# A two-layer decoder trunk: the steps of the mixers in a new order, the first loads and casts rearranged, and a few small operations rewritten

## The chip, the cores and the metric

The kernel runs on one core of a Trainium2 chip. The metric is device time in microseconds (us), the median of several executions. The engines are TensorE (PE, its weight loads PEld), VectorE (DVE), ScalarE (ACT), GpSimd (POOL) and SyncE (SP), which here issues loads and stores.

## The reference

The input is 256 rows of 1024 numbers, all in fp32. Two layers follow each other, each with two sub-layers. With `mod = silu(c) @ w_ada + b_ada`, split into shift, scale and gate for each sub-layer:

```
h = rms_norm(x, g_pre_mix) * (1 + sc1) + sh1
q, k, v, pz = split(h @ w_in)                     # 512 columns each
ao = causal attention, 8 heads of 64, partial rotary (one block of 256)
po = pool_scale * (windowed causal means of pz, minus pz) @ w_pool, 4 groups
y = concat(rms_norm(ao), rms_norm(po)) @ w_out
x = x + gt1 * rms_norm(y, g_post_mix)
h = rms_norm(x, g_pre_ffn) * (1 + sc2) + sh2
a, g = split(causal width-3 conv of (h @ w_up))   # 2816 columns each
x = x + gt2 * rms_norm((silu(a) * g) @ w_down, g_post_ffn)
```

## The kernel before, in words

Rows are in two blocks of 128 (`b` is 0 or 1), columns of a result in two halves (`hf`). Each matmul of full precision is three matmuls of split operands: an operand is cast to a high part (`hi` of a weight, by ACT; `hh` of an activation) and DVE subtracts it from the original for the low part (`lo`, `hl`); `mm3` adds hi*hi, lo*hi and hi*lo.

Weights come through `Stream`: SP issues the loads in one fixed order, each into one of four raw slots of 128 x 2048 numbers, as soon as the slot four units back is free (`pump`, `free`). The parts have eight buffers each for `hi` and `lo` (`high`, `low`, `ahead`). Some weights are not split: the shift and scale columns of `w_ada` (`w_a1`, `w_s2`) are dot products on DVE against `cbc`, the broadcast silu(c); the gate columns (`w_gt`) are matmuls of PE.

The start loads `c` (`row`), x, the identity, the first small vectors and the first weights, all on SP. DVE makes the mean squares of both blocks of x, POOL the power -1/2, DVE the normalised rows `xn`. In `mixer` for layer 0, PE transposes `xn` (`T`), ACT copies the banks to `xT`, and then for each of 8 chunks of 128 input columns `chunk(k)` makes two dot products (`ada1`), a coefficient (`pre_coef`), the casts of the chunk's `w_in` (two parts), and `hh`, `h` and `hl` (`Normed.make`), after which PE runs 24 matmuls (`w_in`). The work of chunk k + 1 stands ahead of the matmuls of chunk k.

`steps` holds what follows in a mixer, as steps of two letters and numbers, issued on each engine in the order of the written list `ORDER[l]`. An engine takes its steps in that order and waits at each for its inputs:

- `cq`, `ck`, `cv`, `cz` copy the projection out of PSUM (a capital letter puts the copy on ACT), `ro` is the rotary (DVE), `kq` transposes (PE), `tq` copies them (`tQ` on ACT);
- `sc` scores (PE), `mx` mask and maximum (DVE), `ex` exponentials (ACT), `rc` and `nm` normalise (DVE; `nM` on ACT), `pt` transposes the probabilities (PE), `cp` copies them (ACT), `at` multiplies with v (PE);
- `wi`, `cd`, `po` are the pooled half (PE, ACT, PE); `mh`, `ml`, `sq`, `sa` split and square both halves; `yP` and `wo` are the output projection of the pooled and the attention half (PE), `cy` copies the former's sum (ACT);
- `ss`, `r1`, `r2` give the two norms' factors (PE, DVE, POOL), `ad` adds the two sums with the factor (DVE), `yq` squares (ACT), `yG` multiplies with factor and gate (DVE), `ry` is the norm's factor (POOL), `xu` updates x (DVE), `xs`, `rx`, `xN` do the same for the next norm (ACT, POOL, DVE), `tr` transposes (PE);
- `gp`, `gq` are the gate and shift columns (PE), `gr`, `gs` copy them, `gc`, `gd` transpose them, `gm`, `gn` add the bias, `gt`, `gg` spread a gate over the rows; `s2` is a dot product (DVE); `hi`, `lo` are casts of weights to come; `tx` and `ts` load ACT's function table for Exp and Silu.

`rstd` on POOL adds eps to the first half's mean square, adds the second half's and takes the power. `ffn` follows, with its own casts, then `tail` (the same chain of norms) and the second layer. The mixer's list ends where the feed-forward net's matmuls (`u`) begin; they need `hl`, `hh` and the first four parts of `w_up`.

Of the kernel before, what the change touches and what calls it, by code (L numbers as in the profile page):

```python
# [76 lines left out]
class Stream:  # L77
# [13 lines left out]
    def add(self, src, n, cuts=()):  # L91
        i = len(self.units)
        self.units.append((src, n))
        self.done.append(False)
        for j, (a, b) in enumerate(cuts):
            self.cut(i, a, b, j == len(cuts) - 1)
        return i
# [4 lines left out]
    def pump(self):  # L102
        while self.loaded < len(self.units):
            src, n = self.units[self.loaded]
            t = None
            if not isinstance(n, int):
                self.nc.sync.dma_start(n, src)
            elif len(self.slots) < RAW_BUFS or self.done[self.slots[-RAW_BUFS]]:
# [54 lines left out]
def trunk(ctx: ExitStack, tc: tile.TileContext, x, c, ct, vec, ident_d, tab_d, w_a1, w_gt, w_s2, w_g2,  # L163
# [80 lines left out]
    for j in range(8):  # L244
        if j:
            add_a1(0, j)
        else:
            A1[0, 0] = [st.add(*h) for h in by_half(w_a1[0, 0])]
# [864 lines left out]
```

## Time and profile before

| | us |
|---|---|
| median of 3 runs (610.43 to 611.44) | 610.45 |
| the profiled execution's own time | 611.41 |
| its span, first to last instruction | 609.6 |
| busy: PE, PEld | 584.1, 504.0 |
| busy: DVE, ACT, POOL | 490.4, 376.7, 29.8 |

Busy time adds up an engine's instructions within the span. Matmuls are pipelined and their ends are modelled, so PE at 96% is not PE at its peak. A line number is that of a helper (L69) for nearly all instructions, so they are told apart by the tiles that they write and read.

### The profile page before, as it was taken

The numbers are of one execution on the slowest core, as the hardware profiler recorded it, in microseconds if no ns is written. First come the engines' busy times: TensorE is split into PE (matmuls) and PEld (weight loads), VectorE is DVE, ScalarE is ACT, GpSimd is POOL, SyncE is SP. The second block draws the span as 40 slices with busy tenths as digits, with TensorE's granted clock in tenths as the row PEclk, the third lists the DMA queues.
The fourth block names the chain that finished last, engine by engine and source line by source line (L and its number), as shares of the span: only waits on it lengthen the run. The fifth ranks groups of instructions, "written<-read, shape, count | busy, mean of one in ns | idle before, by whom it ended". The sixth has DMA issues, their size and how long they took to land.

```text
span 609.6 us, 9688 instructions
## 1 busy us (share of the span) xinstructions
PE 584.1 (96%) x3732; PEld 504.0 (83%) x3732; DVE 490.4 (80%) x865; ACT 376.7 (62%) x664; POOL 29.8 (5%) x62
## 2 busy tenths in 40 slices
PE   5999899699999999999999999979999999999995
PEld 3887567499999999999858876659999999999984
DVE  5998798789999998978559687688989787777753
ACT  4457786777656555557447688768765655656641
POOL 1000100400000000000010000140000000000001
PEclk9999999899999999999999999999999999999999
DMA  8999996667888867864339846765676566455001
GB/s 297 402 395 340 395 366 260 276 210 275 336 297 322 301 262 277 300 236 145 132 114 378 293 145 252 286 228 189 216 280 263 208 215 255 162 197 205 4 1 69
DMA packets 22768, 149.08 MB, mean 245 GB/s; under 512 B 2881, under 2 KB 3265, under 8 KB 6210
## 3 DMA queue, kind: packets, MB, share of 16 engines
q1 hardware_dynamic: 22722, 148.47, 66.0%
q8 instruction: 29, 0.48, 0.3%
q14 instruction: 17, 0.14, 0.1%
HBM read 147.41 MB, written 1.05 MB: 244 GB/s over the span
## 4 chain that ended last, share of the span: by engine, by line
PE 76%; DVE 10%; DMA 5%; ACT 4%; POOL 2%; issue 2%; POOLq 0%; DVEq 0%; SPq 0%; ACTq 0%
PE u L69 41%; PE d L69 20%; PE qk L69 3%; DVE lo L69 3%; PE y L69 2%; DVE raw L69 2%; DMA raw<-w_out_d 2%; PE pz L69 2%; PE v L69 2%; ACT hi L69 1%; DMA raw<-w_in_d 1%; DMA raw<-w_gt_d 1%; PE T L69 1%; POOL rx L69 1%; ACT sqs L69 1%
## 5 line engine op out<-in xcount | busy, mean ns | idle before, releaser
L69 DVE TENSOR_TENSOR lo<-raw,hi 128x1024 fp32r<-128x1024 f32 (+1 forms) x184 | 217.7, 1197 | 29.5 <-ACT hi L69 29.1
L69 ACT CAST hi<-raw 128x1024 fp32r<-128x1024 f32 (+1 forms) x184 | 185.8, 1030 | 58.1 <-DMA raw<-w_in_d 14.8
L69 PE MATMUL u<-hh,hi 128*128 128x256 f32 x704 | 182.2, 282 | 0.3 <-ACT h L69 0.2
L69 PE MATMUL u<-hh,lo 128*128 128x256 f32 x704 | 181.8, 281 | 0.0
L69 PE MATMUL u<-hl,hi 128*128 128x256 f32 x704 | 138.8, 282 | 0.5 <-DVE hl L69 0.5
L69 PEld LDWEIGHTS u<-hh,hi 128*128 128x128 f32 x704 | 132.5, 188 | 2.0 <-ACT hh L69 0.4
L69 PEld LDWEIGHTS u<-hh,lo 128*128 128x128 f32 x704 | 132.5, 188 | 1.4
L69 PEld LDWEIGHTS u<-hl,hi 128*128 128x128 f32 x704 | 107.1, 188 | 1.0 <-DVE hl L69 0.9
L69 DVE SCALAR_TENSOR_TENSOR cv<-u,vecs,cv 128x254 f32<-128x254 f32 (+1 forms) x176 | 83.1, 479 | 26.5 <-ACT cv L69 24.2
L69 ACT ACTIVATE cv<-u,vecs 128x256 f32<-128x256 f32 x88 | 48.7, 558 | 56.0 <-PE u L69 55.9
L69 DVE CUSTOM_DVE_ANT_0 raw<-raw,cbc,vecs 128x1024 f32<-128x1024 f32 x64 | 81.2, 1278 | 1.1 <-DMA raw<-w_g_d 0.9
L69 PE MATMUL d<-hi,sh 128*128 128x512 f32 x176 | 69.7, 396 | 0.0
L69 PE MATMUL d<-lo,sh 128*128 128x512 f32 x176 | 69.2, 393 | 0.0
L69 PE MATMUL d<-hi,sl 128*128 128x512 f32 x176 | 68.6, 394 | 0.0
L69 PEld LDWEIGHTS d<-hi,sl 128*128 128x128 f32 x176 | 33.0, 188 | 7.8 <-DVE sl L69 0.2
L69 PEld LDWEIGHTS d<-hi,sh 128*128 128x128 f32 x176 | 33.1, 188 | 6.6 <-ACT sh L69 0.3
L69 PEld LDWEIGHTS d<-lo,sh 128*128 128x128 f32 x176 | 33.2, 189 | 6.1
L69 ACT CAST sh<-cv 128x256 fp32r<-128x256 f32 x44 | 17.6, 404 | 33.3 <-DVE cv L69 33.3
L69 ACT ACTIVATE cv<-cv 128x256 f32<-128x256 f32 x44 | 18.4, 417 | 17.7 <-DVE cv L69 17.6
L69 ACT ACTIVATE sm<-sm,st 128x128 f32<-128x128 f32 (+1 forms) x52 | 22.0, 448 | 6.6 <-DVE st L69 6.5
L69 DVE TENSOR_TENSOR sl<-cv,sh 128x256 fp32r<-128x256 f32 x44 | 18.4, 421 | 9.1 <-ACT sh L69 9.1
L69 PE MATMUL qk<-hi,hh 128*128 128x512 f32 x64 | 23.0, 419 | 2.9 <-ACT hh L69 2.9
(138 smaller groups left out, 709.6 us busy)
## 6 DMA issues: line engine op xcount, KB each, us to landing
raw<-w_up_d SPq DMA_DIRECT2D x44, 1024.0 KB, 5.0
raw<-w_down_d SPq DMA_DIRECT2D x22, 1024.0 KB, 4.9
raw<-w_gt_d SPq DMA_DIRECT2D x16, 1024.0 KB, 6.6
raw<-w_a_d SPq DMA_DIRECT2D x15, 1024.0 KB, 5.8
raw<-w_out_d SPq DMA_DIRECT2D x8, 1024.0 KB, 6.7
raw<-w_s_d SPq DMA_DIRECT2D x8, 1024.0 KB, 5.5
raw<-w_g_d SPq DMA_DIRECT2D x8, 1024.0 KB, 4.9
raw<-w_in_d SPq DMA_DIRECT2D x6, 1024.0 KB, 6.8
```

Of the source, the lines that this page charges most:

```text
L69: r = op(*a, **k)
```

## The change

- `ORDER` is listed anew for both layers; some steps change engine (`tQ00` to `tq00`, `cz1` to `cZ1`, several `nm`, `ck0` of layer 1 to `cK0`).
- SP's first loads are x and then weights; `row`, `ident` and the first vectors are issued by ACT. The weights of chunk 1 have a place of their own in buffers of the `hi` and `lo` parts (`home`), so those of chunks 0, 1 and 2 are issued at the start. The last chunk's `w_in` takes one raw slot, loaded in two pieces, where it took two.
- The second block's `xn` is made by ACT. PE transposes the first block wholly, then the second; ACT copies one bank ahead of chunk 0 and three behind it (`spread`). The first cast of chunk 0 is shared by ACT and DVE (`high(True)`). PE gets 8 and 12 transposes of the identity whose results are not used (`warm`). The start is kept in written order on all engines (`hold`).
- `rstd` adds a column that holds eps (or 1024 eps) in place of a constant. `r2` takes the power in two pieces and no longer multiplies by 1/32; the factor 32 goes into `gate_cols`, 1024 eps into `ry`. The squares have two scratch tiles. The vectors are laid out in one row for each partition. `wm` is defined and stands in no list.

```diff
 ORDER = [
...
-    "mh1 rc30 nM30 ml1 wo000 sq1 mx20 gq0 mx21 ex20 sa1 wo011 rc20 nm20 ex21 pt30 rc21 wo010 cp30 pt20 nM21 "
-    "wo110 cp20 s221 pt21 nM31 wo001 cp21 s230 pt31 at2 cp31 s231 at3 mh2 sq2 ml2 wo100 sa2 sq3 mh3 wo200 sa3 "
-    "ml3 ss ts gc r1 gm wo101 r2 wo201 gt0 ad10 gt1 gg0 ad11 wo210 gg1 ad00 wo310 ad01 wo300 yG10 hi8 wo301 "
-    "yG00 yq00 wo111 yG01 yq01 wo211 hi9 lo8 wo311 ry0 yq11 xu01 gq1 yq10 yG11 gq2 xs01 xu00 ry1 xs00 gq3 "
-    "xu11 xs11 xu10 rx0 lo9 xs10 gs xN00 xN01 gd rx1 tr00 xN10 gn tr01 xN11 tr10 hi10 tr11 hi11 lo10 lo11",
...
-    "ad11 gt1 wo300 ad01 gg1 ad10 wo301 yq00 wo210 lo15 yq01 gt0 gg0 wo111 ry0 wo211 yG00 xu00 wo311 yG01 "
-    "wo310 yq11 xu01 yq10 gq2 yG10 xs00 yG11 gq3 xs01 ry1 xu11 xs11 xu10 rx0 xN00 xs10 xN01 tr00 gs tr01 gd "
-    "rx1 xN10 xN11 gn tr10 tr11",
+    "pg tx cq0 cq1 ck0 cK1 cv0 ro0 cZ0 ro1 cv1 gp0 cZ1 kq01 kq00 hi0 kq11 tq00 wi0 tQ01 tQ11 sc1 lo0 cd0 po0 "
...
+    "gp3 cy11 mx31 hi6 at1 nm21 yP00 rc20 mh1 ex31 lo6 pt21 ml1 hi7 s200 at0 mh0 sq0 ml0 yP01 gr s201 nM20 "
+    "yP02 sq7 ex30 lo7 wo011 sa7 ts yP03 s210 cy00 wo000 rc31 s211 nM31 pt20 wo001 cp20 rc30 cp21 wo101 nM30 "
+    "at2 sq1 s220 pt30 sq2 s221 pt31 cp30 gc mh2 cp31 wo100 ml2 cy01 sa1 at3 gm sq3 sa2 wo200 mh3 sa3 wo201 "
+    "s230 ss r1 gt1 gt0 s231 gg0 gq0 gg1 ml3 r2 wo010 ad00 wo110 ad01 wo300 ad11 wo301 yq00 yG00 wo111 yq01 "
+    "yG01 wo211 ad10 wo311 ry0 wo210 xu00 yq11 xu01 wo310 xs00 xs01 yG10 gq1 yq10 yG11 gq2 rx0 xN00 xN01 gq3 "
+    "hi8 ry1 tr00 hi9 tr01 xu10 xu11 xs10 gs lo8 xs11 gd lo9 gn rx1 xN10 hi10 xN11 tr10 tr11 hi11 lo10 lo11",
...
+    "wo101 ad00 wo201 ad10 wo300 ad01 wo210 ad11 yq00 wo310 yG00 wo301 yq10 yG10 wo111 yq01 yG01 wo211 wo311 "
+    "ry0 xu01 yq11 gq2 xu00 xs01 gq3 yG11 xs00 ry1 xu10 gs xu11 rx0 xs10 gd xN00 gn xs11 xN01 tr00 tr01 rx1 "
+    "xN10 xN11 tr10 tr11",
 ]
...
-    def add(self, src, n, cuts=()):
+    def add(self, src, n, cuts=(), loads=None, home=None):
         i = len(self.units)
-        self.units.append((src, n))
+        self.units.append((src, n, loads or [(0, n)] if isinstance(n, int) else None, home))
...
-            src, n = self.units[self.loaded]
+            src, n, loads, home = self.units[self.loaded]
             t = None
-            if not isinstance(n, int):
+            if loads is None:
                 self.nc.sync.dma_start(n, src)
+            elif home:
+                t = self.pool.tile([128, 1024], F32R, tag=home, name=home, bufs=PART_BUFS).bitcast(F32)
             elif len(self.slots) < RAW_BUFS or self.done[self.slots[-RAW_BUFS]]:
                 t = self.pool.tile([128, 2048], F32, tag="raw", name="raw", bufs=RAW_BUFS)
-                self.nc.sync.dma_start(t[:, :n], src)
                 self.slots.append(self.loaded)
             else:
                 return
+            for a, b in loads or ():
+                self.nc.sync.dma_start(t[:, a:b], src[:, a:b])
             self.tiles.append(t)
             self.loaded += 1
...
-    def high(self):
+    def high(self, shared=False):
         i, a, b, last = self.queue[len(self.parts)]
         src = self.raw(i)[:, a:b]
         hi = self.pool.tile([128, 1024], F32R, tag="hi", name="hi", bufs=PART_BUFS)
-        self.act.copy(hi[:, :b - a], src)
+        if shared:
+            self.dve.tensor_copy(hi[:, 512:1024], src[:, 512:1024])
+            self.act.copy(hi[:, 0:512], src[:, 0:512])
+        else:
+            self.act.copy(hi[:, :b - a], src)
         self.parts.append((hi, None))
...
+    vflat = vecs.rearrange("p l v -> p (l v)")
...
     for j in range(8):
-        if j:
-            add_a1(0, j)
+        if j == 1:
+            A1[0, 1] = [st.add(*h, home="hi") for h in by_half(w_a1[0, 1])]
+            for h in by_half(w_in0[1]):
+                st.add(*h, [(0, 1024)], home="lo")
         else:
-            A1[0, 0] = [st.add(*h) for h in by_half(w_a1[0, 0])]
-        if 0 < j < NK - 1:
-            st.add(w_in0[j], 2048, half2)
-        else:
-            for h in by_half(w_in0[j]):
-                st.add(*h, [(0, 1024)])
+            A1[0, j] = st.add(w_a1[0, j], 2048, loads=None if j else half2)
+            st.add(w_in0[j], 2048, half2, loads=None if 0 < j < NK - 1 else half2)
...
-    st.load(vecs[:, :, V_GPREF:], vec[:, :, V_GPREF:])
+    st.load(vflat[:, V_GPREF:], vec[:, V_GPREF:])
...
         s0 = 40 if f else 16
         o0 = 24 if f else 16
         g0 = V_GPOSTF if f else V_GPOSTM
-        ve.tensor_mul(coef[l][:, o0:o0 + 8], mod[l][:, s0:s0 + 8], vecs[:, l, g0:g0 + 8])
+        ve.scalar_tensor_tensor(coef[l][:, o0:o0 + 8], mod[l][:, s0:s0 + 8], 1.0 if f else 32.0,
+                                vecs[:, l, g0:g0 + 8], op0=OP.mult, op1=OP.mult)
...
     def mean_sq(src, acc, scale=1.0 / 32.0):
-        t = wk.tile([128, 512], F32, tag="sqs", name="sqs", bufs=1)
+        t = wk.tile([128, 512], F32, tag="sqs", name="sqs", bufs=2)
         se.activation(t[:, :src.shape[1]], src, AF.Square, scale=scale, accum_out=acc)
-    def rstd(ms, name):
+    def rstd(ms, name, eps=1):
         t = small(2, name)
-        ge.tensor_scalar(t[:, 0:1], ms[:, 0:1], EPS, None, op0=OP.add)
+        ge.tensor_tensor(t[:, 0:1], ms[:, 0:1], powc[:, eps:eps + 1], op=OP.add)
...
         if l == 0:
             xT = [w4(f"xT{i}") for i in range(2)]
-            for j in range(NK):
-                for b in range(2):
+            for b in range(2):
+                for j in range(NK):
                     nh.trans(j, b, xn[b])
-                if j % 2:
...
+            def spread(i):
+                se.copy(xT[i // 2][:, (i % 2) * 512:(i % 2 + 1) * 512], nh.T[i])
...
             def chunk(k):
                 ada1(0, k)
                 pre_coef(0, False, k, k + 1)
-                n = 4 if k else 2
-                st.ahead(n - 1)
-                nh.make(k, xT[k // 4][:, (k % 4) * 256:(k % 4 + 1) * 256], True, between=lambda: st.ahead(n))
-            chunk(0)
+                st.ahead(3)
+                nh.make(k, x_of(k), True, between=lambda: st.ahead(4))
+            spread(0)
+            warm(12)
+            ada1(0, 0)
+            pre_coef(0, False, 0, 1)
+            st.high(True)
+            nh.make(0, x_of(0), True, between=st.low)
+            st.high()
+            st.low()
+            for i in (2, 1, 3):
+                spread(i)
+            chunk(1)
+            hold(False)
             for k in range(NK):
-                if k < NK - 1:
+                if 0 < k < NK - 1:
...
         def r2():
             t = r[0]
-            ge.tensor_tensor(t[:, 4:8], t[:, 0:4], powc[:, 0:1].to_broadcast([128, 4]), op=OP.pow)
-            ge.tensor_scalar(t[:, 8:10], t[:, 4:6], 1.0 / 32.0, None, op0=OP.mult)
+            for i in (2, 0):
+                ge.tensor_tensor(t[:, 4 + i:6 + i], t[:, i:i + 2], powc[:, 0:1].to_broadcast([128, 2]), op=OP.pow)
...
-            mean_sq(ys[b, hf], ms[b][:, hf:hf + 1], r[0][:, 8 + b:9 + b])
+            mean_sq(ys[b, hf], ms[b][:, hf:hf + 1], r[0][:, 4 + b:5 + b])
...
         def ry(b):
-            r["y", b] = rstd(ms[b], "ry")
+            r["y", b] = rstd(ms[b], "ry", 2)
...
+    qk0 = [[bank("acc", f"qk{b}{i}") for i in range(2)] for b in range(2)]
+    def warm(n):
+        for i in range(n):
+            te.transpose(qk0[1][1][:, (i % 4) * 128:(i % 4 + 1) * 128], ident, ident)
+    every = (te, ve, se, ge)
...
+    hold(True)
     row = w4("row")[0:1, 0:D]
-    nc.sync.dma_start(row, c)
+    nc.scalar.dma_start(row, c)
     for b in range(2):
         nc.sync.dma_start(xt[b], x[b * 128:(b + 1) * 128, :])
-    nc.sync.dma_start(ident, ident_d)
-    nc.sync.dma_start(vecs[:, :, 0:V_GPREF], vec[:, :, 0:V_GPREF])
+    nc.scalar.dma_start(ident, ident_d)
+    nc.scalar.dma_start(vflat[:, 0:V_GPREF], vec[:, 0:V_GPREF])
     ge.memset(ones, 1.0)
     ge.memset(powc[:, 0:1], -0.5)
-    ge.memset(powc[:, 1:2], 0.5)
+    ge.memset(powc[:, 1:2], EPS)
+    ge.memset(powc[:, 2:3], D * EPS)
     ge.memset(dummy, 0.0)
...
-    xn = []
+    warm(8)
+    xn, r0 = [w4(f"xn{b}") for b in range(2)], [small(2, "r0") for b in range(2)]
     for b in range(2):
-        t = small(2, "r0")
-        xn.append(w4(f"xn{b}"))
         ve.tensor_tensor_reduce(xn[b], xt[b], xt[b], 1.0 / D, EPS, op0=OP.mult, op1=OP.add,
-                                       accum_out=t[:, 0:1])
-        ge.tensor_tensor(t[:, 1:2], t[:, 0:1], powc[:, 0:1], op=OP.pow)
-        ve.tensor_scalar(xn[b], xt[b], t[:, 1:2], None, op0=OP.mult)
+                                accum_out=r0[b][:, 0:1])
+        ge.tensor_tensor(r0[b][:, 1:2], r0[b][:, 0:1], powc[:, 0:1], op=OP.pow)
+    ve.tensor_scalar(xn[0], xt[0], r0[0][:, 1:2], None, op0=OP.mult)
+    se.activation(xn[1], xt[1], AF.Copy, scale=r0[1][:, 1:2])
...
-        "pool_out_gain", "pool_scale", "conv_w", "conv_b")], axis=2)
+        "pool_out_gain", "pool_scale", "conv_w", "conv_b")], axis=2).reshape(128, L * V_N)
```

## Rows read from the trace of the kernel before

**Rows 1.** The busy time by stage: the stretch in us from the span's start, its length, then busy time (and instructions) of PE, PEld, DVE, ACT and POOL, the granted TensorE clock, the DMA engines' busy share and GB/s.

```profile
0.00:16.00 16.00, 9.37 (x25) 5.90 (x26) 8.76 (x13) 7.70 (x11) 2.65 (x10) 1.00 0.84 300
16.00:60.50 44.50, 44.50 (x192) 35.76 (x191) 39.71 (x67) 26.46 (x37) 0.00 (x0) 1.00 0.98 379
60.50:109.00 48.50, 45.88 (x285) 31.89 (x284) 41.25 (x113) 37.41 (x92) 4.34 (x6) 1.00 0.85 325
109.00:121.50 12.50, 7.92 (x53) 5.38 (x52) 9.21 (x16) 9.83 (x21) 6.51 (x12) 0.86 0.83 330
121.50:308.50 187.00, 186.93 (x1322) 175.07 (x1323) 162.63 (x261) 110.28 (x176) 2.18 (x7) 1.00 0.70 252
...
350.00:405.50 55.50, 54.63 (x309) 40.54 (x307) 43.99 (x114) 42.34 (x101) 6.38 (x8) 1.00 0.59 219
405.50:416.50 11.00, 7.34 (x47) 5.18 (x46) 8.58 (x16) 8.72 (x21) 4.04 (x9) 0.84 0.58 227
```

**Rows 2.** Instructions of the start in order of time, all engines mixed: start us, us, engine, line, operation, out<-in, count; in brackets the idle time before and what ended it.

```profile
1.14 0.83 SPq L1002 DMA_DIRECT2D x<-x_d  x2
...
7.45 1.57 DVE L69 TENSOR_SCALAR xn<-x,r 128x1024 f32<-128x1024 f32 x2 [0.43 <-POOL r L69]
...
8.26 3.68 PE L69 MATMUL T<-ident,xn 128*128 128x128 f32 x16 [2.22 <-DVE xn L69]
8.94 1.28 DVE L69 CUSTOM_DVE_ANT_0 raw<-raw,cbc,vecs 128x1024 f32<-128x1024 f32 x1
...
10.05 2.50 ACT L69 COPY xT<-T 128x512 f32<-128x512 f32 x4 [3.38 <-PE T L69]
...
12.45 1.05 ACT L69 CAST hi<-raw 128x1024 fp32r<-128x1024 f32 x1
13.40 0.60 ACT L69 ACTIVATE hh<-xT,mod,coef 128x256 fp32r<-128x256 f32 x1
...
14.05 2.08 PE L69 MATMUL qk<-hi,hh 128*128 128x512 f32 x4 [2.12 <-ACT hh L69]
...
16.45 1.28 DVE L69 CUSTOM_DVE_ANT_0 raw<-raw,cbc,vecs 128x1024 f32<-128x1024 f32 x1
...
17.62 0.39 PE L69 MATMUL v<-hi,hh 128*128 128x512 f32 x1
...
17.85 0.39 PE L69 MATMUL pz<-hi,hh 128*128 128x512 f32 x1
```

**Rows 3.** The same view inside and at the end of the loop over the chunks: the first dot product of chunks 2 and 7, the `hh` of chunk 7, and PE's last matmul of the loop.

```profile
22.46 1.28 DVE L69 CUSTOM_DVE_ANT_0 raw<-raw,cbc,vecs 128x1024 f32<-128x1024 f32 x1
...
50.78 1.28 DVE L69 CUSTOM_DVE_ANT_0 raw<-raw,cbc,vecs 128x1024 f32<-128x1024 f32 x1
...
53.38 0.60 ACT L69 ACTIVATE hh<-xT,mod,coef 128x256 fp32r<-128x256 f32 x1 [0.30 <-DVE coef L69]
...
60.15 0.40 PE L69 MATMUL pz<-hi,hl 128*128 128x512 f32 x1
```

**Rows 4.** What PE waited for, of the stretch 60.4 to 109 (two rows) and of 350 to 405.5 (two rows): total us, times, longest.

```profile
PE gacc L69 <- DMA raw<-w_gt_d: 1.8, 2, 1.5
PE sc L69 <- ACT k L69: 0.7, 1, 0.7
...
PE gacc L69 <- ACT pts L69: 0.6, 1, 0.6
PE pT L69 <- DVE sm L69: 0.2, 1, 0.2
```

**Rows 5.** The second `w_out` load: the stretch 55 to 70 in the columns of rows 1, and the load's issue on SP and its cast on ACT in the columns of rows 2.

```profile
55.00:70.00 15.00, 13.29 (x80) 9.20 (x78) 9.03 (x21) 10.45 (x17) 0.00 (x0) 1.00 1.02 420
...
55.64 0.33 SPq L110 DMA_DIRECT2D raw<-w_out_d  x1
...
67.98 1.99 ACT L69 CAST hi<-raw 128x1024 fp32r<-128x1024 f32 x2 [1.88 <-DMA raw<-w_out_d]
```

**Rows 6.** The ends of the two tails, in the columns of rows 2: DVE's last two low parts of the first, its wait for the transposed shift columns and the next two low parts in the second.

```profile
118.83 2.35 DVE L69 TENSOR_TENSOR lo<-raw,hi 128x1024 fp32r<-128x1024 f32 x2
...
413.47 0.17 DVE L69 TENSOR_TENSOR mod<-gT,vecs 128x8 f32<-128x8 f32 x1 [0.66 <-PE gT L69]
...
413.75 2.36 DVE L69 TENSOR_TENSOR lo<-raw,hi 128x1024 fp32r<-128x1024 f32 x2
```

**Rows 7.** The load of ACT's function table in the first mixer, in the columns of rows 2.

```profile
99.53 1.28 ACT L69 ACT_TABLE_LOAD   x1
```

**Rows 8.** POOL's additions for the norms, and DVE beside one of them, in the columns of rows 2; the two rows at 303 and 304 are of the feed-forward net's tail.

```profile
107.78 1.21 DVE L69 TENSOR_TENSOR lo<-raw,hi 128x1024 fp32r<-128x1024 f32 x1
108.14 0.93 POOL L69 TENSOR_SCALAR ry<-msy 128x1 f32<-128x1 f32 x1 [4.70 <-ACT sqs L69]
...
303.61 0.22 POOL L69 TENSOR_SCALAR rx<-msx 128x1 f32<-128x1 f32 x1 [1.69 <-ACT sqs L69]
304.43 0.19 POOL L69 TENSOR_TENSOR rx<-rx,msx 128x1 f32<-128x1 f32 x1 [0.59 <-ACT sqs L69]

```

**Rows 9.** DMA issues of the first 15 us: target and source, queue, count, KB each, us from issue to landing.

```profile
x<-x_d SPq DMA_DIRECT2D x2, 512.0 KB, 3.8
...
raw<-w_in_d SPq DMA_DIRECT2D x2, 512.0 KB, 6.8
```

More of the change, by code (lines that the diff above doesn't have):

```diff
@@ L203, in trunk @@
     ones = cst.tile([128, 1], F32, name="ones")
-    powc = cst.tile([128, 2], F32, name="powc")
+    powc = cst.tile([128, 3], F32, name="powc")
     dummy = cst.tile([128, 1], F32, name="dummy")
@@ L308, in ada1 @@
     def ada1(l, j):
-        if l or j:
+        if l or j != 1:
             dots(l, A1[l, j], (8 + j, j))
         else:
-            for i, ch in zip(A1[0, 0], (8, 0)):
+            for i, ch in zip(A1[0, 1], (9, 1)):
                 dots(0, i, (ch,))
@@ L477, in mixer @@
         pz = None
-        qk = [[bank("acc", f"qk{b}{i}") for i in range(2)] for b in range(2)]
+        qk = [[bank("acc", f"qk{b}{i}") for i in range(2)] for b in range(2)] if l else qk0
         vps = None
@@ L492, in mixer, with x_of @@
             xT = [w4(f"xT{i}") for i in range(2)]
-            for j in range(NK):
-                for b in range(2):
+            for b in range(2):
+                for j in range(NK):
                     nh.trans(j, b, xn[b])
-                if j % 2:
-                    se.copy(xT[j // 4][:, (j % 4 - 1) * 256:(j % 4 + 1) * 256], nh.T[j // 2])
             vps = [bank("ps", f"v{b}") for b in range(2)]
             pz = [bank("ps", f"pz{i}") for i in range(2)]
+            def spread(i):
+                se.copy(xT[i // 2][:, (i % 2) * 512:(i % 2 + 1) * 512], nh.T[i])
+            def x_of(k):
+                return xT[k // 4][:, (k % 4) * 256:(k % 4 + 1) * 256]
             def chunk(k):
@@ L774, in r1 @@
         def r1():
-            t = r[0] = small(10, "ra", 1)
+            t = r[0] = small(8, "ra", 1)
             ve.tensor_scalar(t[:, 0:4], srcs["ss"][:, 0:4], 1.0 / 512.0, EPS, op0=OP.mult, op1=OP.add)
@@ L874, in number, with wm @@
             return 10 * n[0] + n[1] if len(n) > 1 else n[0]
+        def wm(n):
+            p = bank("ps", "wm")
+            for i in range(16):
+                te.transpose(p[:, (i % 4) * 128:(i % 4 + 1) * 128], ident, ident)
         def tx():
@@ L996, in ffn, with hold @@
         return tail(mms, acc, gate, store if l + 1 == L else None)
+    qk0 = [[bank("acc", f"qk{b}{i}") for i in range(2)] for b in range(2)]
[3 more added lines that the diff above has]
+    every = (te, ve, se, ge)
+    def hold(on):
+        for e in every:
+            e.held = on
+    hold(True)
     row = w4("row")[0:1, 0:D]
-    nc.sync.dma_start(row, c)
+    nc.scalar.dma_start(row, c)
     for b in range(2):
         nc.sync.dma_start(xt[b], x[b * 128:(b + 1) * 128, :])
-    nc.sync.dma_start(ident, ident_d)
-    nc.sync.dma_start(vecs[:, :, 0:V_GPREF], vec[:, :, 0:V_GPREF])
+    nc.scalar.dma_start(ident, ident_d)
+    nc.scalar.dma_start(vflat[:, 0:V_GPREF], vec[:, 0:V_GPREF])
     ge.memset(ones, 1.0)
     ge.memset(powc[:, 0:1], -0.5)
-    ge.memset(powc[:, 1:2], 0.5)
+    ge.memset(powc[:, 1:2], EPS)
+    ge.memset(powc[:, 2:3], D * EPS)
     ge.memset(dummy, 0.0)
```

24 rows, old and new, of the table ORDER are left out of this document.

## Prediction

> **What bounds the kernel now.** I read the busy time by stage first [rows 1]. Columns after the stretch: its length, then busy time and instruction count of PE, PEld, DVE, ACT, POOL, then granted clock, DMA share, GB/s. Seven stretches tell the story. The feed-forward net of a layer takes 187 us in which PE is busy for 186.93: nothing in it is edited, so it moves as a block. What can change is the 121.5 us ahead of it and the 108 us from 308.5 to 416.5, above all the mixers' list (48.5 and 55.5 us) and the tails behind the last output-projection matmul (12.5 and 11.0 us). In the first 16 us PE is busy for 9.4, partly at slow spacing; from 16.0 to 60.5 it is full, 192 matmuls in 44.5 us, 0.232 us each.
>
> Second, the order of instructions in the start [rows 2]: DVE squares both halves of x, both normalised halves are made on DVE by 9.0, the two dot products of the first chunk follow at 8.94, the first cast waits until 12.45 because ACT copies all four transposed banks first, and the first matmul comes at 14.05. Its four take 2.08 us, over twice 0.232 apiece; the granted clock reads 1.00 there, but at the start the matmul spacing is that of the lower level (1.2 GHz), and it is down to 0.23 only some 3.5 us later (17.62, 17.85).
>
> Third, the loop over the eight chunks [rows 3]: the dots of chunk 2 begin at 22.46 and those of chunk 7 at 50.78, so DVE and ACT turn a chunk in 5.66 us while PE needs 24 x 0.232 = 5.57. PE ends at 60.4, one chunk after the last `hh` at 53.38 and a bit: it still pays off its late start.
>
> Fourth, waits of PE by cause [rows 4]: in the first mixer's list only 1.8 us for gate weights and 0.7 for the transposed keys, in the second 0.6 named. So PE itself fills both lists, 46.0 of 48.5 us in the first. The chain of waits there runs through a load, though: the second `w_out` piece is issued at 55.64, cast at 67.98, with the DMA engines full from 55 to 70 [rows 5]; until it is there the matmuls of the pooled half can't begin.
>
> Last, the tails: PE idles there for the norm chain, which alternates ACT, POOL and DVE, and steady matmuls begin only after two casts of DVE behind `xN` [rows 6].
>
> **The change: the start.** SP issues x first, 0.42 us earlier than 1.14, as the three small loads go to ACT's queue (before the first Silu ACT only loads a table). DVE finishes the first normalised half at 7.8 (7.45 and half of 1.57, less 0.42); the other goes to ACT, priced by the cast of equal size, 1.05 us, so 7.85 to 8.9. DVE's dots of chunk 0 then run 7.8 to 10.4 instead of 8.94 to 11.6, the coefficient to 10.5 and the shared half cast, which the trace does not show, between 0.3 (a quarter of a whole subtraction's 1.21 us [rows 8], for half the elements and one input of two) and 0.6 (half of it): I take 0.6, to 11.1. PE transposes eight blocks of the first half from 7.85 at 0.23 (3.68 / 16) and two of the second by 10.2; only one bank copy (0.6) is left ahead of ACT's half cast (0.6), and `hh` (0.6) ends at 12.0. Low parts and the second cast follow: `lo` 11.4 to 12.6, `hl` to 13.0, second cast 12.5 to 13.5, second `lo` to 14.7. So the dots of chunk 1 begin at 14.7, not 16.45. Its loads no longer wait for slots: with one chunk more in the parts' buffers and another in raw slots, all issued by 6.8, w_in of chunk 1 (5.2 MB into the stream) is there by some 15.5 at 400 GB/s, between the 379 of the loop [rows 1] and the 420 of later [rows 5]. With a normal 5.66 in place of 6.0 for that chunk, chunk 2 begins at 20.4 instead of 22.46: DVE is 2.0 us ahead. `hh` of chunk 7 comes at 51.4, and PE could end at 51.4 + 0.5 + 5.57 = 57.4.
>
> PE must also start early enough: from X it needs 8 x 5.57 = 44.6. The twelve extra transposes stand in its queue ahead of the first matmul, after 16 that end near 11.5. At 0.23 they end at 14.3, at the 0.12 of a warm PE at 13.0. X = 14.3 gives 58.9, X up to 12.8 gives 57.4. PE idles less ahead of X in the new order (eight transposes more fill the hole ahead of x), so I expect the faster spacing near X and take 57.7: **2.7 us** earlier than 60.4, bounds 1.5 and 3.0. The DMA page of the Trainium skill ("DMA: Bandwidth & Descriptors", section on queues, rings and completion order) speaks against hoping for more: SP's and ACT's rings lie on the same 16 engines, which take turns between them. No run here shows ACT's queue yet; by that rule the small loads cost x about their own bytes, 0.12 MB or 0.3 us at 400 GB/s (an estimate).
>
> **The first mixer.** Chunk 7's w_in is one slot instead of two, so the gate and `w_out` loads move up one place: they wait for the slots of chunks 6 and 7, which DVE frees 2 us earlier and one unit earlier each. Counting from the slots at 2.6 us for each MB I put `w_out`'s second piece at about 62 instead of 67.98 [rows 5]. In the new list its first cast, `hi2`, has twelve ACT steps ahead of it; the last ones need `po1`, which PE ends 9.5 us into its list, and then come `sq5`, `mh4` and others: 11 us after PE leaves the input projection, 68.7. So it has 6 us to spare, and the 1.8 us wait for gate weights goes too, as does 0.7 for the keys (copied at once by ACT and DVE: `tq00` beside `tQ01`). Against this, the Silu table load `ts` now stands on ACT ahead of `cp20`, `cp21` and `cp31`, with 1.28 us [rows 7], where before it came behind all of them; PE's `at2` and `at3` are queued behind those copies, and the `wo` steps behind them. Following ACT's list from `hi7` I find `cp21` ending about 0.8 us after PE is free for `at2`, and `cp31` 0.5 after it is free for `at3` (estimates; the 1.28 is the largest part). PE's list: 2.5 taken away, 1.3 added, **1.2 us** less; bounds: 2.5 less, and nothing less.
>
> The tail. After the last `wo` come `yq10` (now behind `xs00`, `xs01` on ACT), `ry1` (now behind `rx0` on POOL), `xu10`, `xu11`, `xs`, `rx1`, `xN`, two `lo`s, `hl`. The first half's chain is finished earlier, but the last half's is as long as before and gets two neighbours more; `lo8` and `lo9` fill DVE's wait for `rx1`. Counted from the last `wo`: `yq10` ends after 2.4 us, `ry1` at 4.4, `xu11` (0.7 each) at 5.8, `xs11`, with `gs` ahead of it, at 7.3, `rx1` at 9.0, as `lo9` holds POOL up, `xN11` at 9.9, `lo11` at 12.2, and steady matmuls begin at 12.7 where it is 12.5 now: **0.2 us lost**, bounds 1.5 either way.
>
> **The second mixer.** PE's named waits (0.8) go, none of the new order is visibly worse, **0.8 us** less. In its tail `gn` moves from behind `xN11` to between `xN00` and `xN01`; today DVE waits about 0.7 us for it and then makes two `lo`s at 413.75 [rows 6]. Against it, `rx1` waits once for an `xu`. I count **0.5 us**, bounds 0 and 1.4.
>
> **eps, 1/32, scratch.** A POOL add of a constant takes 0.22 us where DVE is quiet, the add of two columns 0.19 [rows 8]. The first half of the tail shows the same constant add at 0.93, and it ends as the 1.21 us `lo` next to it does: POOL stood still for DVE. The page "SBUF — State Buffer" of the Trainium skill, section on who interferes with whom, has a rule for it: a DVE instruction with two SBUF inputs excludes a GpSimd one that reads SBUF, whichever of them began first. By it the new add of two columns is blocked just the same, and the edit gains nothing; by the face value of 0.93 against 0.19 it would gain 0.7 at each of two places on the chain, 1.4 in all. I take 0 because the two rows differ by what runs beside them, 1.4 is the upper bound. Dropping the multiplication by 1/32 spares POOL a step behind the power, which `ad` does not wait for: 0; at most the 0.22 of such a step, should `yq` wait for it. The second scratch tile is written by ACT alone, in order: 0.
>
> Sum: 2.7 + 1.2 - 0.2 + 0.8 + 0.5 = 5.0 us. The profiled execution took 611.41 us (span 609.6), so 606.4; the median of the runs is 610.45, 0.96 below it, so I expect 605.4.
>
> **Rivals.** *The start alone* (0.20): the relisted mixers stall where I see no wait, because lists without slack give back 2 us: 607.5 to 609. For it: DVE is busy for 41 of 48.5 us in the first list and its steps stand in one row, so one late ACT result holds all that follow. Against: the removed waits are real.
>
> *PE without gaps* (0.14): start 3.0, both lists at PE's own time (2.5 and 0.8), tails shortened by 1.5 and 1: 601.6. For it: PE's clock is granted at 0.86 and 0.84 in the tails [rows 1]; with `tr00`, `tr01` ahead of `gd` PE idles in shorter pieces. Against: steady matmuls wait for `lo`, not for PE.
>
> *No change* (0.05): the loads set the pace. If `w_out` landed only as early as the DMA's idle share before 16 us allows (16% of 16 us, 2.6 us), the cast would start at 65.4, still ahead of 68.7; it decides only from there.
>
> *Slower* (0.11): seven megabytes in flight share the engines instead of queueing. Then w_in of chunk 0, alone with 3 MB today, lands with the rest, 17 us after the first issue rather than within 6.8 us of its own [rows 9]; the first cast moves from 12.45 to about 18, the loop ends 5.5 us later, and after 2.3 us from the mixers 613.7 is left. It decides once w_in lands later than about 15. Against: x, issued first, lands in 3.8, w_in behind it in 6.8, so today transfers finish in their order.
>
> The forecast has 0.50. Below 601.6 or above 609.3 I leave 0.18, so the range is 601.6 to 609.3. A difference under 0.2% (1.2 us) can't be told from none here: faster 0.84, same 0.05, slower 0.11.
>
> **What would show it.** First qk matmul near 13 with four in about 1 us; dots of chunk 1 near 14.7; last pz matmul at 57 to 58; casts of `w_out` without a DMA wait; PE's waits for `w_gt` gone and one at `ao` for `pts` of about 1 us; last `wo` at 104 to 105.5; first steady `u` at 117 to 118; the second layer's list 54.7 us long, its tail 10.5. The prediction fails if x lands later than 4.6, if the first matmul isn't before 14, or if a wait of more than 1.5 us shows up on PE between 58 and 104.

## The result and the profile after

The changed kernel takes 602.81 us (median; 602.25 to 603.6) beside 610.87 for the kernel before in the same runs: ratio 0.987, 95% interval 0.9852 to 0.9888, 8.1 us less. A second series of the same kernel gave 603.41 beside 610.49, ratio 0.9882 (0.9869 to 0.9894), 7.1 less. The forecast was 605.4, 5.0 less, in a range down to 601.6: the sign and the range held, the gain was undersized by 2 to 3 us.

The busy time by stage of the kernel after, in the columns of [rows 1]. The first cut is here at the first matmul of the input projection (in [rows 1] at 16.0, some 2 us behind it), the others are at the same events as there:

```profile
0.00:12.05 12.05, 9.64 (x41) 7.13 (x41) 6.35 (x12) 5.39 (x8) 1.96 (x11) 1.00 0.86 308
12.05:58.70 46.65, 46.36 (x198) 35.78 (x197) 42.09 (x69) 29.30 (x42) 0.00 (x0) 1.00 1.00 400
58.70:105.30 46.60, 46.33 (x287) 32.12 (x287) 41.10 (x113) 37.09 (x93) 6.61 (x9) 1.00 0.85 322
105.30:116.30 11.00, 7.46 (x52) 4.95 (x52) 9.74 (x16) 9.22 (x19) 4.31 (x9) 0.84 0.83 317
...
344.40:398.20 53.80, 53.80 (x309) 40.29 (x307) 44.64 (x117) 42.42 (x102) 7.92 (x9) 1.00 0.67 235
398.20:406.60 8.40, 6.26 (x39) 4.48 (x39) 7.54 (x13) 6.95 (x16) 3.45 (x9) 0.80 0.66 252
```

The first two stages together end at 58.7 where they ended at 60.5, and every later stage with an edit in it is shorter. The row of the second list holds the first lesson: PE runs 309 instructions in it, as in [rows 1], but is busy 53.80 us where it was 54.63. The old 54.63 held short pauses between one matmul's start and the next that the profile counts as busy.

All that PE still waits for in the whole run (total us, times, longest), and the share of each engine in the chain of work that ended last:

```profile
PE cb L69 <- DMA row<-c_d: 2.4, 1, 2.4
PE T L69 <- DVE xn L69: 2.2, 1, 2.2
PE gT L69 <- ACT grow L69: 2.1, 2, 1.4
PE T L69 <- DVE mod L69: 1.4, 1, 1.4
PE qk L69 <- ACT hh L69: 0.8, 1, 0.8
PE y L69 <- DVE y L69: 0.3, 1, 0.3
PE v L69 <- ACT hi L69: 0.2, 1, 0.2
```

```profile
PE 91%; DVE 3%; ACT 3%; issue 1%; POOL 1%; DMA 0%; DVEq 0%; POOLq 0%; ACTq 0%
```

The waits for gate weights and keys of [rows 4] are gone; only the `y` row lies in a mixer's list, the `xn`, `grow` and `mod` rows lie in the tails.

The start, in the columns of [rows 2]:

```profile
8.72 1.28 DVE L69 CUSTOM_DVE_ANT_0 raw<-raw,cbc,vecs 128x1024 f32<-128x1024 f32 x1 [1.15 <-DMA vecs<-vec_d]
...
11.39 0.60 ACT L69 ACTIVATE hh<-xT,mod,coef 128x256 fp32r<-128x256 f32 x1
12.05 1.20 PE L69 MATMUL qk<-hi,hh 128*128 128x512 f32 x4
13.48 0.49 PE L69 MATMUL v<-hi,hh 128*128 128x512 f32 x1 [0.23 <-ACT hi L69]
14.60 1.28 DVE L69 CUSTOM_DVE_ANT_0 hi<-hi,cbc,vecs 128x1024 f32<-128x1024 f32 x1
...
14.93 0.50 PE L69 MATMUL pz<-hi,hh 128*128 128x512 f32 x1
...
16.18 0.40 PE L69 MATMUL qk<-lo,hh 128*128 128x512 f32 x1
...
19.25 1.28 DVE L69 CUSTOM_DVE_ANT_0 raw<-raw,cbc,vecs 128x1024 f32<-128x1024 f32 x1 [0.94 <-DMA raw<-w_a_d]
```

The first matmul comes 2.0 us earlier and its four take 1.20. The next ones stand 0.49 apart, the lower clock level, until 15.3; from 16.18 on they stand 0.24 apart or less.

### The profile page after: what moved, and what is told of

It reads as the page before. It is cut to its first block, busy times and chain, and to the rows that moved or that the text cites. A ratio compares the mean times of both kernels' runs of the same rounds, so it can differ in the third digit from the quotient of the medians.

```text
span 600.5 us, 9728 instructions
## 1 busy us (share of the span) xinstructions
PE 585.0 (97%) x3752; PEld 504.9 (84%) x3752; DVE 490.4 (82%) x868; ACT 374.3 (62%) x662; POOL 29.8 (5%) x63
## 4 chain that ended last, share of the span: by engine, by line
PE 91%; DVE 3%; ACT 3%; issue 1%; POOL 1%; DMA 0%; DVEq 0%; POOLq 0%; ACTq 0%
PE u L69 42%; PE d L69 20%; PE qk L69 6%; PE yp L69 4%; PE y L69 3%; PE v L69 3%; PE pz L69 3%; PE gacc L69 2%; PE T L69 2%; DVE lo L69 1%; PE sc L69 1%; PE ao L69 1%; ACT hi L69 1%; PE pT L69 1%; ACT sqs L69 1%
## 5 line engine op out<-in xcount | busy, mean ns | idle before, releaser
L69 ACT CAST hi<-raw 128x1024 fp32r<-128x1024 f32 (+1 forms) x182 | 183.8, 1030 | 50.8 <-PE u L69 13.9
L69 DVE CUSTOM_DVE_ANT_0 raw<-raw,cbc,vecs 128x1024 f32<-128x1024 f32 x62 | 79.2, 1287 | 3.5 <-DMA raw<-w_g_d 1.4
L69 ACT ACTIVATE sm<-sm,st 128x128 f32<-128x128 f32 (+1 forms) x48 | 20.7, 453 | 3.4 <-DVE st L69 3.1
```

Source lines behind the costliest of these rows:

```text
L69: r = op(*a, **k)
```

## The experiments

One profile of each kernel is not enough for stages of this size, so the table puts all of them side by side; each entry is read from PE's and DVE's instructions in order of time. "Free" is the time at which PE has issued the last matmul of the stage (its start plus 0.23): of the input projection, then of the first list. The tail columns count from there to the first `hl` on DVE and to the first `d` matmul of the feed-forward net; from that one on the net took 166.9 to 167.2 us (layer 0) and 168.5 to 168.7 (layer 1) in all of them.

| kernel | first matmul | free of input proj. | free of list 0 | tail 0: to hl / to d | list 1 | tail 1: to hl / to d |
|---|---|---|---|---|---|---|
| before | 14.05 | 60.4 | 108.9 | 12.2 / 32.5 | 55.6 | 10.6 / 29.2 |
| sqs_two | 14.12 | 61.7 | 108.9 | 11.9 / 32.3 | 55.6 | 10.5 / 29.1 |
| eps_only | 14.92 | 62.3 | 109.6 | 11.3 / 32.2 | 55.6 | 9.8 / 28.4 |
| lists_only | 14.58 | 62.0 | 109.1 | 10.8 / 32.4 | 53.8 | 9.2 / 28.3 |
| old_lists | 12.15 | 59.2 | 106.0 | 11.5 / 31.9 | 55.6 | 9.9 / 28.6 |
| old_list0 | 12.35 | 59.5 | 105.7 | 11.5 / 31.9 | 53.7 | 8.9 / 28.0 |
| old_list1 | 11.96 | 59.3 | 105.9 | 10.7 / 31.8 | 55.9 | 9.4 / 28.0 |
| old_eps | 11.35 | 58.5 | 105.6 | 10.8 / 31.8 | 53.7 | 9.1 / 27.9 |
| after | 12.05 | 58.6 | 105.2 | 10.6 / 30.9 | 53.8 | 8.5 / 27.5 |
| after_again | 12.23 | 59.1 | 105.7 | 10.6 / 32.2 | 54.0 | 8.5 / 27.1 |
| no_warm | 11.86 | 59.0 | 105.6 | 10.6 / 32.0 | 53.7 | 8.5 / 27.1 |
| warm_tail | 11.84 | 58.9 | 105.5 | 10.6 / 30.9 | 54.1 | 8.5 / 27.1 |
| vecs_first | 14.07 | 60.1 | 106.7 | 10.6 / 31.1 | 53.7 | 8.5 / 27.5 |

**Which part pays: the lists put back.** Three kernels from after, with written lists of before in place:

```
old_lists:  ORDER = [before[0], before[1]]
old_list1:  ORDER = [after[0],  before[1]]
old_list0:  ORDER = [before[0], after[1]]
```

> The kernel after with both written lists of before: the start and the small operations stay new. Theory A (each stage is worth what its end moved by between the two traces: start 1.8 us, first mixer 3.5, second mixer 3.7, small operations nothing): 610.9 - 1.8 = 609.1, and the input projection ends near 58.6 as in after. Theory B (the prediction's sizes: start 2.7, first mixer 1.0, second 1.3): 608.2. Theory C (the surplus of 3 us over the forecast comes from the rewritten small operations): 606 to 607.

> The kernel after with the second mixer's list of before alone. Theory A: 602.8 + 3.7 = 606.5, the whole loss between 344 and 416, list near 55.5 and tail near 11. Theory B: 602.8 + 1.3 = 604.1. Theory C (the tail got shorter through the small operations, whatever the list): 603.6 to 604.1, with a tail that stays near 8.5.

> The kernel after with the first mixer's list of before alone. Theory A: 602.8 + 3.5 = 606.3, all of it before 121. Theory B: 602.8 + 1.0 = 603.8. Rival D (the new start frees DMA slots earlier, so the old list no longer waits for the second w_out piece): the old list alone gets shorter by about 1 us, 605.

Measured 606.99 (ratio to before 0.9945, 0.9924 to 0.9966), 606.17 (0.9941, 0.9917 to 0.9964) and 604.39 (0.9901, 0.988 to 0.9922). The second list is worth 606.17 - 602.81 = 3.4 us (2.8 against the second series of after, and 606.99 - 604.39 = 2.6 with the old first list), nearer to theory A than to B; the table puts 1.8 us into the list itself (55.6 to 55.9 us with the old one, 53.7 to 54.1 with the new), the rest into its tail. The first list is worth 0.8 to 1.6 by the times, less than theory A, and the intervals overlap, so the times alone do not show it; inside the list the table shows 0.3 on average (PE free at 106.0 and 105.7 with the old list, 105.2 to 105.9 with the new). Rival D holds there: the old list behind the new start is 46.2 to 46.9 us long, as short as the new one's 46.6, and its casts wait for `w_out` 0.2 us at most, where they waited 3.6 in the profile of before. PE still waits there for gate weights, 1.0 us in old_lists and 0.6 in old_list0.

**The lists alone**, in the kernel before:

```
-ORDER = [before[0], before[1]]
+ORDER = [after[0], after[1]]
```

> The kernel before with both new written lists and nothing else. Theory E (the first mixer's list got shorter through the new start, which frees DMA slots earlier, and the second's through its order): first list no shorter than before, 48.5 us or a little more because it waits for loads, its tail 0.8 shorter; second list 2.0 shorter, tail 0.5 to 1 shorter: 610.2 - 3.5 = 606.7. Theory A (each list is worth its own stage): first list 2 us shorter too, 604.7. Theory B (the prediction's sizes: 1.0 and 1.3): 607.9.

It took 607.7 (0.9946, 0.9929 to 0.9964). By the time that is nearest to theory B, but the stages are those of theory E. The first list ends at 109.1, as with the old one (108.9 to 109.6), the second takes 53.8. Its input projection ended 1.6 us later than in the profile of before, and the list took it back: 108.9 to 109.6 comes out of four starts that lie 1.9 us apart. A PE that enters the old list early waits there longer for gate weights (1.8 us in [rows 4], 0.7 and 0.8 in sqs_two and eps_only); in the new list of lists_only it waits for none.

**The small operations**, first put back into after (old_eps, with the step of 1/32 and the one scratch tile, whose lines are not shown), then two of them brought into before one at a time:

```
old_eps, in after:
-ge.tensor_tensor(t[:, 0:1], ms[:, 0:1], powc[:, eps:eps + 1], op=OP.add)
+ge.tensor_scalar(t[:, 0:1], ms[:, 0:1], EPS, None, op0=OP.add)
...
eps_only, in before:
-ge.tensor_scalar(t[:, 0:1], ms[:, 0:1], EPS, None, op0=OP.add)
+ge.tensor_tensor(t[:, 0:1], ms[:, 0:1], epsc[:, 0:1], op=OP.add)
sqs_two, in before:
-t = wk.tile([128, 512], F32, tag="sqs", name="sqs", bufs=1)
+t = wk.tile([128, 512], F32, tag="sqs", name="sqs", bufs=2)
```

> The kernel after with the constant add of eps, the 1/32 step and one scratch tile as before; lists and start stay new. Theory A and the prediction: no more than 0.4 us slower, 602.8 to 603.2. Theory C: 1.4 us (the upper bound named in the prediction) to 3 us slower, 604.2 to 606, all of it in the two tails, and POOL's constant add of 0.9 us on the chain there.

> The kernel before with the add of a column that holds eps in place of POOL's add of a constant, and nothing else. The prediction: 0, since the new add is held up by DVE in the same places (blocked adds of 0.5 to 0.9 us stay on POOL). Rival C (the constant form itself is slow beside DVE): 0.7 at each of two places, 1.4 less, 608.8, with every add of the column at 0.2.

> The kernel before with two scratch tiles for the squares and nothing else. The prediction: no difference (0). Theory F (two squares into one tile stand 0.81 to 0.87 us apart, into two tiles 0.61 to 0.68): 0.15 to 0.2 for each pair on the chain, two or three pairs in a tail, so each tail 0.3 to 0.6 shorter, 0.6 to 1.2 in all, 609 to 609.6.

Old_eps took 604.26 (0.9904, 0.9887 to 0.9921), 0.9 to 1.5 more than after; the two ratios' intervals overlap. eps_only 610.13 (0.9998, 0.9985 to 1.0011) and sqs_two 610.81 (1.0003, 0.9989 to 1.0017) are no change. POOL in the first tail of eps_only:

```profile
108.81 0.92 POOL L69 TENSOR_TENSOR ry<-msy,epsc 128x1 f32<-128x1 f32 x1 [4.72 <-ACT sqs L69]
...
112.05 0.75 POOL L69 TENSOR_TENSOR ry<-msy,epsc 128x1 f32<-128x1 f32 x1 [1.41 <-ACT sqs L69]
```

The first is the place where the constant add took 0.93 [rows 8]: the rewritten add is held up just the same, so rival C falls, and the trace agrees with the rule quoted in the prediction (the Trainium skill, "SBUF — State Buffer", who interferes with whom). Not every place is alike, though. The first add of the next norm in this tail, in before and then in eps_only, with DVE beside it:

```profile
113.14 1.41 DVE L69 SCALAR_TENSOR_TENSOR x<-yg,ry,x 128x512 f32<-128x512 f32 x2 [1.03 <-POOL ry L69]
113.19 0.78 POOL L69 TENSOR_SCALAR rx<-msx 128x1 f32<-128x1 f32 x1
```

```profile
113.66 0.19 POOL L69 TENSOR_TENSOR rx<-msx,epsc 128x1 f32<-128x1 f32 x1
113.72 1.42 DVE L69 SCALAR_TENSOR_TENSOR x<-yg,ry,x 128x512 f32<-128x512 f32 x2 [0.98 <-POOL ry L69]
```

The add that began 0.05 us behind DVE took 0.78, the one that began 0.06 ahead of it 0.19. In this tail the `hl` of eps_only comes 0.6 to 0.9 us sooner than in sqs_two and before (11.3 to 11.9 and 12.2), of which 0.1 to 0.3 is left at the first `d`; that is one profile, and the times show no gain. In sqs_two the squares of a pair do move together, but POOL's next add is then caught instead: 0.22 for the constant, 0.74 for the sum behind it.

```profile
111.02 0.22 POOL L69 TENSOR_SCALAR ry<-msy 128x1 f32<-128x1 f32 x1 [1.11 <-ACT sqs L69]
111.33 0.74 POOL L69 TENSOR_TENSOR ry<-ry,msy 128x1 f32<-128x1 f32 x1
```

The table gives eps_only 0.8 us in the second tail; that is PE's clock and not the edit. The same eight transposes of before, then of eps_only:

```profile
410.64 1.94 PE L69 MATMUL T<-ident,xn 128*128 128x128 f32 x8 [3.18 <-DVE xn L69]
```

```profile
411.37 1.07 PE L69 MATMUL T<-ident,xn 128*128 128x128 f32 x8 [3.17 <-DVE xn L69]
```

The last `xN`, which the edit could move, ends 7.3 us behind the last `wo` in before, eps_only and sqs_two alike. With the two edits together it ends at 6.9 in the old order (old_lists, old_list1), and in the new one at 6.3 (after, after_again) where old_eps has 6.9. So each alone is worth nothing in this second tail, both together 0.4 to 0.6. (The step of 1/32 changes along with them in these kernels; it was not run by itself.)

**How much one profile can tell: the same kernel again.**

```
(no edit)
```

> The changed kernel once more, beside the same runs of before as the three that follow. Theory: ratio 0.987 again, some 602 to 603, with the stretches of its trace within 0.3 us of the first profile; if a stretch differs by more, that much of any stage difference is not the edit.

The median is 603.41, as above, and the stretches are not all within 0.3: from the last `wo` to the first `d` it takes 32.2 us where the first profile shows 30.9, though the `hl` comes 10.6 behind in both. The stretches 113.5 to 116.5 and 116.5 to 119.5 of the first profile, then of the second, in the columns of [rows 1]:

```profile
113.50:116.50 3.00, 3.00 (x17) 3.00 (x16) 3.00 (x5) 2.48 (x6) 0.00 (x0) 0.56 1.02 426
116.50:119.50 3.00, 3.00 (x28) 3.00 (x27) 1.34 (x4) 3.00 (x7) 0.00 (x0) 1.00 0.91 289
```

```profile
113.50:116.50 3.00, 2.70 (x13) 2.70 (x14) 3.00 (x5) 2.25 (x6) 0.00 (x0) 0.50 1.02 429
116.50:119.50 3.00, 3.00 (x16) 3.00 (x16) 1.71 (x5) 3.00 (x7) 0.00 (x0) 0.50 1.05 311
```

PE idled ahead of this in the tail (2.2 us for `xn`), the granted clock stands at one half, 1.2 GHz, and how long it stays there differs: it is back before 116.5 in one, only after 119.5 in the other. The Trainium skill ("TensorE: Matmul & The Clock Gate", section on the HAM clock gate) says that activity releases the throttle and that the number of slow matmuls differs between runs of one kernel; the two traces agree, 1.3 us apart.

**The tail without PE's idling.** Extra transposes of the identity in the two idle stretches; they write parts of T that are written again before they are read:

```
+def wt(*n):
+    for i in range(number(n)):
+        te.transpose(nh.T[i % 4][:, 128:256], ident, ident)
-tr01 xu10 xu11 xs10 gs lo8 xs11 gd lo9
+tr01 wt10 xu10 xu11 xs10 gs lo8 xs11 gd wt16 lo9
```

> The changed kernel with 10 and 16 extra transposes of the identity in PE's two idle stretches of the first mixer's tail (behind tr01 and behind gd); they write parts of T that tr10 and tr11 overwrite. Theory G (in the changed kernel PE runs the first u matmuls at the lower clock level because it idled in the tail: 20.3 and 21.6 us from the first hl to the first down matmul in its two profiles, 18.7 to 19.1 in the second tail): the granted clock stays 1.00, u at 0.12 spacing from the start, 19 to 19.5 us there, 0.4 to 2 us less in all, 601.5 to 603. Rival (the low parts set the pace there, not the clock): no change, 603.4, or slower if the transposes run late and hold tr10.

It took 602.44 (0.9865, 0.9846 to 0.9884), the lowest median of all, but against after the times alone do not settle it. The granted clock of the same stretches is 1.00:

```profile
113.50:116.50 3.00, 2.30 (x16) 1.87 (x16) 3.00 (x5) 2.47 (x6) 0.00 (x0) 1.00 1.02 429
116.50:119.50 3.00, 2.86 (x24) 2.86 (x25) 1.70 (x5) 2.88 (x7) 0.00 (x0) 1.00 0.85 314
...
116.64 0.74 PE L70 MATMUL u<-hl,hi 128*128 128x256 f32 x4 [0.70 <-DVE hl L70]
```

Theory G holds as far as the clock goes, and so, in part, does the rival: at the full clock PE waits 0.70 for `hl`, so the stretch from `hl` to `d` is 20.3 and not the 19 to 19.5 expected. To `d` it is 30.9, 1.1 to 1.3 less than in no_warm and after_again, and no better than in the lucky first profile.

**The start's two doubtful pieces.** The extra transposes left out; and the vectors ahead of the identity on ACT's queue, with 4 transposes for 12:

```
no_warm:
-    warm(8)
-            warm(12)
vecs_first:
-    nc.scalar.dma_start(ident, ident_d)
     nc.scalar.dma_start(vflat[:, 0:V_GPREF], vec[:, 0:V_GPREF])
+    nc.scalar.dma_start(ident, ident_d)
-            warm(12)
+            warm(4)
```

> The changed kernel without the 8 and the 12 extra transposes at the start. If they do what I priced them for (the faster spacing near the first matmul): first matmul still near 12.0, but its four at 2 us and slow spacing for some 3 us more, input projection ends 0.7 to 1.5 later (59.9 to 60.7) and the end comes as much later at most, 604.1 to 604.9. Rival (the first chunk loses its 1.4 us either way, because the clock falls back at 13.3 in spite of them): no change, 603.4.

> The changed kernel with the small vectors ahead of the identity on ACT's queue and 4 extra transposes in place of the 12. Theory H (the late vectors cost DVE 1.15 us ahead of the first dots, and the first matmul with them): dots at 7.6 instead of 8.7, first hh at 10.4 to 10.8, first matmul near 11.3, input projection 0.5 to 0.8 earlier. Rival (the transposes and the lower clock level set the first matmul, not the dots): first matmul not before 11.8 and no change of the end; or the identity lands late now, and the transposes of x with it.

no_warm took 603.24 (0.9875, 0.9855 to 0.9896), no change against after. The four first matmuls do take 2.07 instead of 1.20 and the slow spacing lasts until 17, yet the input projection ends at 59.0 as with them; the next section shows why. vecs_first took 604.85 (0.9904, 0.9885 to 0.9922), 1.4 to 2.0 us slower. The vectors land at 5.5 instead of 8.6 and the dots start at 7.75, but now the identity takes 6.6 us instead of 4.5, and PE stands still for it ahead of all transposes:

```profile
8.28 1.97 PE L69 MATMUL qk<-ident 128*128 128x128 f32 x8 [1.95 <-DMA ident<-ident_d]
...
14.07 1.20 PE L69 MATMUL qk<-hi,hh 128*128 128x512 f32 x4 [0.41 <-ACT hh L69]
```

Theory H falls: whichever load is second on that queue is late, and the identity costs more. What would pay is left open: both loads ahead of the big ones weren't tried.

## Why the prediction was right, and where it was off

Means over the profiles of the table that share a part; the first number is the forecast's.

**Start: 2.7, measured 2.6 at the end of the input projection.** Four old starts end at 61.6 on average, seven new ones (without no_warm and vecs_first) at 59.0. That the size fits is luck: the forecast counted from the 60.4 of one profile and expected 57.7, and from 60.4 the seven gain 0.9 to 1.8 only. The single pair of profiles says 1.8, because the profile of before was the luckiest of its kind: its first matmuls left the lower clock level sooner (0.23 apart from 17.62 [rows 2]; in sqs_two 0.43 at 17.7). The landmarks held: dots of chunk 1 at 14.60 (14.7 forecast), x landed at 4.14, first matmul 12.05 (near 13). The end did not, 58.5 to 59.5 instead of 57.7. PE's first chunk takes 6.93 us (its first matmul at 12.05, the next chunk's at 18.98) in place of 5.57, since the fast spacing I expected from X on is lost again between 13.3 and 15.3. But that does not set the end: in no_warm the first chunk takes 7.91, and the end is 59.0 too. What the forecast had wrong is the end of its sum, 51.4 + 0.5 + 5.57. In all seven new starts PE is free 6.90 to 6.92 us behind the `hh` of chunk 7, not 6.07, because it pauses in that chunk for `hl`, which DVE makes only behind the chunk's two `lo`. The rows of after, in the columns of [rows 2]:

```profile
53.83 0.42 DVE L69 TENSOR_TENSOR hl<-h,hh 128x256 fp32r<-128x256 f32 x1
53.86 0.39 PE L69 MATMUL qk<-lo,hh 128*128 128x512 f32 x1
...
54.30 0.96 PE L69 MATMUL qk<-hi,hl 128*128 128x512 f32 x3
```

From 53.86 to 54.30 is 0.44 where the matmuls of this loop stand 0.23 apart, a pause that the waits view does not list, and 18 of the chunk's 24 matmuls are still to come. In no_warm PE arrives later and finds `hl` ready, so it loses no more than 0.3 at the end. The `hh` of chunk 7 itself comes at 51.63 to 52.54, not 51.4: in the seven, DVE waits 0.94 to 1.46 us for the `w_a` load of chunk 2 (the row at 19.25 above).

The vectors were the term I had no row for: 6.9 us to landing, where before they took 3.8 on SP's queue, and 1.15 us of DVE's time ahead of the first dots. What that is worth at the end is not shown, as DVE waits for chunk 2's load later in any case.

```profile
ident<-ident_d ACTq DMA_DIRECT2D x1, 64.0 KB, 4.5
vecs<-vec_d ACTq DMA_DIRECT2D x1, 28.0 KB, 6.9
```

x itself landed as before, 3.9 against 3.8 [rows 9]. The page "DMA: Bandwidth & Descriptors" of the Trainium skill (section on queues, rings and completion order) has the rings of SP and ACT share the same engines; these rows fit that, but it is the small loads that paid and not x.

**First list: 1.2, measured 0.3 (105.85 to 105.6); with the start 3.9 forecast and 3.5 measured.** The waits did go, and those for `w_out` too, but the list is no shorter for its order: the old list behind the new start is as short, with 0.6 and 1.0 us of waits for gate weights left in it. Less its named waits the old list takes 45.6 to 45.9 us (before, old_list0, old_lists), the new one 46.3, so what the new order saves in waits it spends between PE's matmuls, where no wait is named (24 `pT` take 2.67 us from start to start and took 2.34). The wait of 0.8 and 0.5 for `cp20`, `cp21` and `cp31` behind the table load never came: PE's waits show none, and `at2` and `at3` start 0.33 us behind the `wo` matmul ahead of them. Taking 1.8 us of waits as the list's own was the error: a PE that arrives 1.3 us later (sqs_two) waits 1.1 less.

**First tail: -0.2, measured +0.6 to the first `d` (32.4 to 31.7).** Its chain got 1.5 shorter (12.2 to 10.6), not longer: I counted from `yq10`, but in the new order block 0 is finished ahead of the end, `xN00` at 106.8, 1.6 us behind the last `wo`, where it was at 116.15, 7.2 behind. `rx1` is indeed held up by `lo8` and `lo9`, as forecast. Most of the gain is given back by PE at the lower clock level; warm_tail, at the full clock, keeps all of it (30.9 to the first `d`).

**Second list: 0.8, measured 1.8.** The step that failed is the price "PE's named waits (0.8) go". The waits view names only gaps; the rest sat inside the busy time (of the 1.76 us that the list lost, 0.87 were gaps and 0.83 busy time). One of the largest such pieces, eight `sc` matmuls in before and then the same in after:

```profile
358.53 1.25 PE L69 MATMUL sc<-k,q 64*128 64x128 f32 x8
```

```profile
352.76 0.93 PE L69 MATMUL sc<-k,q 64*128 64x128 f32 x8
```

No idle time is shown ahead of either, but the old eight take 0.32 us more. The other three groups of eight take 0.93 in both, and the rest of the 0.83 is spread over smaller pieces of other matmuls.

**Second tail: 0.5, measured 1.9 (29.2 to 27.3, without eps_only and its faster clock).** lists_only has 0.9 of it, nearly twice what I gave the move of `gn`; some of the rest is the small operations, **eps, 1/32, squares: 0**, which are worth 0.4 to 0.6 here together, inside their bound of 1.4. The mechanism forecast for the add alone held, that DVE beside it decides and not its form; "the second scratch tile: 0" did not, since a pair of squares stands 0.15 closer with it, and what that gives is kept only where POOL's next add isn't caught by DVE instead. How much is the clock's was not separated.

Sum of the stages: 3.5 + 0.6 + 1.8 + 1.9 = 7.8, against 7.1 to 8.1 measured. The forecast's range held, but of its 5.0 the start's size fits by luck, and the 2 to 3 us that it lacks are the second list (1.0) and the two tails (0.8 and 1.4), less 0.4 that start and first list fell short of. Of the rivals, PE without gaps had the tails right (2.5, and 2.5 measured), but gave the start and the first list 5.5, where 3.5 came, and the second list 0.8; slower and no change had no support, w_in landed within 7.8 us of its issue.

## What to carry to other kernels

Price a list on an engine that is "busy" by comparing the time of equal instructions, from start to start, with their normal spacing, for short pauses are not in the waits. A wait that goes is not yet a gain: a new order can spend it elsewhere, and an earlier load can end it too; only putting one part back at a time shows which. Ask at the end of a stage what its last instructions wait for, and count the time from there. Shorten a tail's idle time and look at the granted clock behind it: one profile can be off by more than the edit.

## What was not expected of the hardware

Of the same program, the stretch at the lower clock level after the first tail lasted until 116.2 us in one profile and 119.6 in another. The level rose in the start, then fell again between 13.3 and 15.3 us with PE idle for 0.23 us only; no run here explains that. A load of 28 KB, third on ACT's queue, took 6.6 to 6.9 us to land while 64 KB ahead of it took 4.3 to 4.5, and with their order changed the times changed places.
